# A hybrid encoder step on one core: the first query block's low products, the engines of the low parts, and the last norm

## The chip, the core and the metric

The kernel runs on one core of a Trainium2 chip. Its engines are TensorE (PE in the rows; PEld is its weight load), VectorE (DVE), ScalarE (ACT), GpSimd (POOL) and SyncE (SP), which here only issues transfers. The metric is the time of one execution on the device in microseconds; less is better.

## What is computed

One layer of a streaming encoder: 1024 prompt tokens and 128 sample tokens go through one projection to the queries, keys and values of three kinds of attention and to a gate; M is attention into 256 memory tokens, A is banded, B differential. The mixed result is gated, projected by `w_out`, added to the input and normalised.

```python
a_q, a_k, a_v, b_q, b_k, b_v, m_q, gate = split(x @ w_in)
mk, mv = split(mem_prompt @ w_mem_kv)
o_a, o_b, o_m = band(a_q, a_k, a_v), diff(b_q, b_k, b_v), memory(m_q, mk, mv)
y = (concat(o_a, o_b, o_m) * silu(gate)) @ w_out
out = layer_norm(2 ** 0.25 * x + y, g, b)      # mean and variance over 1024 features
```

## The kernel before

Every large product is made of three products of rounded numbers: an operand is split into a high part, its copy rounded to the type of the matrix product, and a low part, the rest. A product is then high by high, low by high and high by low. `step` (L154 to L157) issues these three for one of the eight slices of 128 features, `k`: L155 is x's high part with the weights' high part, L156 x's **low** part with the weights' high part, L157 x's high part with the weights' low part. ScalarE makes the high parts (a cast), VectorE or GpSimd the low parts (a subtraction).

The 1152 tokens (prompt, then sample) are three chunks of 384: `xh[c]` and `xl[c]` are x's high and low parts of chunk `c` (the last two slices of chunk 0 are in tiles named `rh` and `rl`). `load_x` (L241) brings a chunk in four transfers of two slices each, into six buffers `xr`; a buffer is free for a later transfer when both the cast and the subtraction of its slices are done. In the text these low parts are xl0a to xl0d, xl1a to xl1d and xl2a to xl2d, in the order of their transfers (xl0d is `rl`). `XP` sends the second and the fourth of each chunk to GpSimd, the others to VectorE.

The program starts with the memory's keys and values: `load_mem_w` (L221) loads and splits their weights and the memory tokens (`memr`, in the `xr` buffers too), `mem_block` (L249) makes four blocks of 256 columns. `split_mem` (L192) then splits the first unit's keys (into `ka`, `kl`) and values (`va`); its three subtractions are VectorE's.

Then comes the first query block, M0's: `q_of(units[0])` gives three chunks of eight steps; after the last step of a chunk `evac` moves the result out of its PSUM buffer `pp` (two of these) into `qa`, by ScalarE (L168) and VectorE (L172) in turn, half by half. While M0's attention runs, the projection of the next block (B0's queries, by the same `step`) fills TensorE.

A scheduler sets the order of the instructions on each engine by a model of their times; inside a `manual_schedule` block the named engine keeps the order of the code, and `high_priority` moves instructions ahead by a number of places. An engine works off its order strictly, so an instruction that waits holds up all behind it on its engine.

SyncE issues x's transfers, the next weights (`wraw`), the stores of the memory's keys and values, the tables `cos` and `sin`, and `dlam` (L307), 128 KB into a tile `t` that takes the room of what was loaded early. VectorE's row L310 works on that tile and stands ahead of the maxima (L766) that M0's softmax begins with.

At the end seven output tiles of 128 tokens follow one another: eight slices of `products` per cut, then `add` (L1052) with its statistics and `norm` (L1065). For the last tile, `t == 8`, there is nothing behind the norm to hide it: VectorE works on columns 0 to 799 (L1077, L1088); columns 800 to 1023 go to ScalarE (L1084, with a `bias` that VectorE makes first at L1083) and then through two operations of GpSimd (L1085, L1086). Both parts wait for `rstd`, a power on GpSimd (L1073). Two transfers of SyncE (L1090) store them.

## Time and profile before

| | |
|---|---|
| median of 3 runs | 676.22 us (675.5 to 677.12) |
| the profiled execution, its own time | 675.73 us |
| its span, first to last instruction | 673.9 us |
| TensorE busy | 660.9 us, 98% of the span |
| VectorE, ScalarE, GpSimd busy | 70%, 53%, 35% |
| mean granted TensorE clock | 0.996 |

The profiled execution's own time is 1.8 us above its span. In the rows below a line is: start, duration, engine, line of the kernel, operation, what it writes from what it reads, shapes and count; in square brackets the idle time of the engine ahead of it and what ended that. The busy time of TensorE is that of pipelined matrix products with modelled ends, so a product of 384 columns is shown with 0.34 us though the next starts 0.17 us later; starts are the better measure.

### The profile page before, as it was taken

Reading aid. Unit: us, or ns where it says so; the run is one execution under the profiler, and the core shown is the slowest. Engines: PE = TensorE matmul, PEld = TensorE weight load, DVE = VectorE, ACT = ScalarE, POOL = GpSimd, SP = SyncE. Lnnn points to the kernel's source line nnn. Section 1 sums busy time; section 2 is a strip of 40 time slices with the busy share of each in tenths; the row PEclk is TensorE's granted clock in tenths of the full one; section 3 lists DMA queues with packets and bytes.
Section 4 is the critical chain, followed back from the end, with each engine's and each line's share of the span. In section 5 each row is a group of like instructions: output and inputs, shape, how many; then the busy total and the mean of one; then the engine's idle time right before and its main releaser. Section 6 shows DMA issues by size and latency. Waiting matters only on the chain.

```text
span 673.9 us, 12216 instructions
## 1 busy us (share of the span) xinstructions
PE 660.9 (98%) x4306; PEld 614.8 (91%) x4306; DVE 473.7 (70%) x1169; ACT 356.3 (53%) x922; POOL 235.1 (35%) x282
## 2 busy tenths in 40 slices
PE   9899999999999999999999999999999999999995
PEld 8899999999999999999999999999999998887884
DVE  4869966796569856898466516675376689897854
ACT  6748855566455655566465635666466577211000
POOL 8654212541344333541234234313324124153101
PEclk9999999999999999999999999999999999999998
DMA  8771442022312222023322122031322657974411
GB/s 279 236 226 52 143 140 72 33 80 75 96 58 83 75 100 75 25 97 127 94 68 71 52 95 75 25 118 62 127 87 95 211 173 243 318 268 148 157 62 63
DMA packets 55693, 78.91 MB, mean 117 GB/s; under 512 B 9368, under 2 KB 33232, under 8 KB 55632
## 3 DMA queue, kind: packets, MB, share of 16 engines
q1 hardware_dynamic: 55632, 78.13, 35.4%
q8 instruction: 34, 0.56, 0.3%
q14 instruction: 27, 0.22, 0.1%
HBM read 57.69 MB, written 20.42 MB: 116 GB/s over the span
## 4 chain that ended last, share of the span: by engine, by line
PE 85%; DVE 7%; DMA 4%; issue 1%; ACT 1%; SPq 1%; POOL 0%; POOLq 0%; DVEq 0%; ACTq 0%
PE pp L155 16%; PE pp L156 16%; PE pp L157 16%; PE pp L1049 8%; PE ps L1049 6%; PE pt L476 4%; PE po L639 4%; PE ps L463 4%; PE ps L464 4%; PE po L678 3%; PE pt L891 1%; PE ps L806 1%; DVE xl L219 1%; DVE p L545 1%; PE pt L427 1%
## 5 line engine op out<-in xcount | busy, mean ns | idle before, releaser
L155 PE MATMUL pp<-xh,whi 128*128 128x384 f32 x616 | 211.5, 343 | 0.2 <-DVE qa L172 0.2
L156 PE MATMUL pp<-xl,whi 128*128 128x384 f32 x616 | 209.8, 341 | 1.8 <-DVE xl L219 1.8
L157 PE MATMUL pp<-xh,wlo 128*128 128x384 f32 x616 | 209.8, 341 | 0.0
L156 PEld LDWEIGHTS pp<-xl,whi 128*128 128x128 f32 x616 | 115.9, 188 | 4.6 <-DVE xl L219 2.4
L155 PEld LDWEIGHTS pp<-xh,whi 128*128 128x128 f32 x616 | 115.9, 188 | 3.2 <-issue 0.7
L157 PEld LDWEIGHTS pp<-xh,wlo 128*128 128x128 f32 x616 | 115.9, 188 | 1.6 <-issue 0.2
L140 POOL TENSOR_TENSOR wlo<-wraw,whi 128x512 fp32r<-128x512 f32 x54 | 72.4, 1362 | 65.6 <-ACT whi L139 50.4
L605 ACT ACTIVATE p<-ps,nm 128x512 f32<-128x512 f32 (+3 forms) x96 | 55.2, 580 | 47.8 <-DVE nm L602 36.2
L463 PE MATMUL ps<-ka,qa 128*128 128x512 f32 (+4 forms) x176 | 58.7, 339 | 0.5 <-DVE nm L712 0.5
L464 PE MATMUL ps<-kl,qa 128*128 128x512 f32 (+4 forms) x176 | 57.5, 328 | 0.0
L476 PE MATMUL pt<-ident,p 128*128 128x128 f32 x332 | 54.9, 274 | 0.6 <-DVE p L545 0.5
L600 DVE TENSOR_REDUCE nm<-ps 128x1 f32<-128x512 f32 (+3 forms) x96 | 51.0, 549 | 1.6
L480 DVE TENSOR_TENSOR ptl<-pt,pth 128x512 fp32r<-128x512 f32 x56 | 38.3, 684 | 10.3 <-ACT pth L479 9.7
L479 ACT CAST pth<-pt 128x512 fp32r<-128x512 f32 x56 | 32.6, 587 | 23.1 <-PE pt L476 19.9
L720 POOL TENSOR_SCALAR p<-p,rs 128x640 f32<-128x640 f32 (+4 forms) x32 | 21.5, 676 | 64.3 <-DVE rs L719 58.7
L476 PEld LDWEIGHTS pt<-ident,p 128*128 128x128 f32 x332 | 39.7, 141 | 3.9 <-DVE p L545 0.8
L1049 PE MATMUL pp<-xh,whi 128*128 128x512 f32 (+1 forms) x96 | 36.5, 381 | 0.0
L1049 PE MATMUL pp<-xl,whi 128*128 128x512 f32 (+1 forms) x96 | 36.2, 377 | 0.0
L1049 PE MATMUL pp<-xh,wlo 128*128 128x512 f32 (+1 forms) x96 | 35.9, 378 | 0.0
L639 PE MATMUL po<-pth,va 128*128 128x256 f32 (+1 forms) x160 | 35.4, 285 | 0.0
L463 PEld LDWEIGHTS ps<-ka,qa 128*128 128x128 f32 x176 | 33.2, 189 | 2.0 <-DVE nm L712 0.7
L484 DVE TENSOR_TENSOR ptl<-pt,pth 128x256 fp32r<-128x256 f32 (+1 forms) x72 | 25.1, 352 | 13.6 <-ACT pth L483 13.0
(240 smaller groups left out, 1425.0 us busy)
## 6 DMA issues: line engine op xcount, KB each, us to landing
wraw<-in_win SPq DMA_DIRECT2D x54, 256.0 KB, 3.2
xr<-in_xT SPq DMA_DIRECT2D x12, 384.0 KB, 4.6
gates<-t SPq DMA_DIRECT2D x24, 192.0 KB, 2.1
qa<-in_xn SPq DMA_DIRECT2D x9, 512.0 KB
out_y<-qa SPq DMA_DIRECT2D x16, 256.0 KB, 2.3
mixed<-od SPq DMA_DIRECT2D x28, 128.0 KB, 1.8
p<-gates SPq DMA_DIRECT2D x7, 512.0 KB
p<-mixed SPq DMA_DIRECT2D x7, 448.0 KB
```

The lines of the kernel that those rows point to most:

```text
L140: eng.tensor_tensor(out=lo[:, h], in0=raw, in1=f(hi[:, h]), op=ALU.subtract)
L155: nc.tensor.matmul(ps, lhsT=w[0][:, k], rhs=xh_[:, k], start=(k == 0), stop=False)
L156: nc.tensor.matmul(ps, lhsT=w[0][:, k], rhs=xl_[:, k], start=False, stop=False)
L157: nc.tensor.matmul(ps, lhsT=w[1][:, k], rhs=xh_[:, k], start=False, stop=(k == KT - 1))
L463: nc.tensor.matmul(ps, lhsT=u.qa[h][:, qs], rhs=u.ka[h][:, k0 : k0 + n], start=True, stop=False)
L464: nc.tensor.matmul(ps, lhsT=u.qa[h][:, qs], rhs=kl[h][:, k0 : k0 + n], start=False, stop=True)
L476: nc.tensor.transpose(pt[:, t, q * P : (q + 1) * P], p[q][:, cols[t][q] : cols[t][q] + P], ident)
L480: nc.vector.tensor_tensor(out=lo, in0=pt, in1=f(hi), op=ALU.subtract)
L600: nc.vector.tensor_reduce(out=nm[:, m, c : c + 1], in_=ps[c][:, : b - a], axis=AX.X, op=ALU.max, negate=True)
L605: nc.scalar.activation(e[:, a:b], ps[c][:, : b - a], AF.Exp, bias=nm[:, m, 0:1], accum_out=rs[:, m, c : c + 1])
L639: nc.tensor.matmul(out, lhsT=a, rhs=b, start=(g == 0 and x == 0), stop=(g == j and x == len(mm) - 1))
L1049: nc.tensor.matmul(y, lhsT=a[:, k], rhs=b[k][:, s], start=(k == 0 and x == 0), stop=(k == KT - 1 and x == 2))
```

## The change

There are three edits.

1. The first query block gets a function of its own, `q_first`. For each chunk it issues first the sixteen products with x's high part (`high`), and the eight with its low part (`low`) after the sixteen of the next chunk. Its third chunk has its PSUM buffer from the pool `ps_s` (three buffers, for scores), so that all three exist at once. Each of the two is a `manual_schedule` block of its own; between blocks the scheduler decides.
2. All twelve low parts of x are VectorE's, with a high priority. The three subtractions of the first memory keys and values go to GpSimd. The first transfer of the memory tokens is issued by ScalarE, not SyncE.
3. The last norm is cut into columns 0 to 383, 384 to 767 (VectorE) and 768 to 1023: there VectorE takes the mean off and multiplies by the gain, ScalarE multiplies by `rstd`, GpSimd adds; ScalarE issues the store of that part, SyncE the other two. The `bias` goes.

```diff
-XP = [2, 6]
-LS = 800
+XPR = 200
+LS = [(0, 384), (384, 768)]
...
-    def split_mem(u, kv, v):
+    def split_mem(u, kv, v, eng=nc.vector):
...
-        split_k(kv, 256, u.ka, kl, 0)
+        split_k(kv, 256, u.ka, kl, 0, eng)
...
-        nc.vector.tensor_tensor(out=u.va[:, :, :, 64:128], in0=v, in1=f(u.va[:, :, :, 0:64]), op=ALU.subtract)
+        eng.tensor_tensor(out=u.va[:, :, :, 64:128], in0=v, in1=f(u.va[:, :, :, 0:64]), op=ALU.subtract)
...
-                    nc.sync.dma_start(memr, d["memT"][:, 256 * a : 256 * b].rearrange("p (k c) -> p k c", c=256))
+                    (nc.sync if i else nc.scalar).dma_start(memr, d["memT"][:, 256 * a : 256 * b].rearrange("p (k c) -> p k c", c=256))
...
-                split_part(xh[c], xl[c], xr, a, a + 2, nc.gpsimd if a in XP else nc.vector)
+                with tc.high_priority(offset=XPR):
+                    split_part(xh[c], xl[c], xr, a, a + 2, nc.vector)
...
+    def q_first(u):
...
+        ps = [ps_p.tile([P, CH], F32, tag="pp") for _ in range(2)] + [ps_s.tile([P, 512], F32, tag="ps")[:, 0:CH]]
+        def high(c):
+            with tc.manual_schedule(engines={PE}):
+                for k in range(KT):
+                    for i in range(2):
+                        nc.tensor.matmul(ps[c], lhsT=w[i][:, k], rhs=xh[c][:, k], start=(k == i == 0), stop=False)
+        def low(c):
+            with tc.manual_schedule(engines={PE}):
+                for k in range(KT):
+                    nc.tensor.matmul(ps[c], lhsT=w[0][:, k], rhs=xl[c][:, k], start=False, stop=(k == KT - 1))
+            with tc.high_priority(offset=HP):
+                evac(c, ps[c])
+        high(0)
+        for c in range(1, 3):
+            high(c)
+            low(c - 1)
+        low(2)
...
-            bias = small.tile([P, 1], F32, tag="ri")
-            nc.vector.scalar_tensor_tensor(out=bias, in0=mv[:, 0:1], scalar=-1.0, in1=rstd, op0=ALU.mult, op1=ALU.mult)
-            nc.scalar.activation(z[:, s], z[:, s], AF.Identity, bias=bias, scale=rstd)
-            nc.gpsimd.tensor_tensor(out=z[:, s], in0=z[:, s], in1=norms[0][:, s], op=ALU.mult)
-            nc.gpsimd.tensor_tensor(out=z[:, s], in0=z[:, s], in1=norms[1][:, s], op=ALU.add)
...
+            nc.scalar.activation(z[:, rest], z[:, rest], AF.Copy, scale=rstd)
+            nc.gpsimd.tensor_tensor(out=z[:, rest], in0=z[:, rest], in1=norms[1][:, rest], op=ALU.add)
...
+        if last:
+            nc.scalar.dma_start(o["y"][t, :, rest], z[:, rest])
```

TensorE, where chunk 0 of the first query block ends (`pp_453` is chunk 0's result, `pp_508` before and `pp_454` now chunk 1's; `whi` and `wlo` are the weights' parts). Before:

```order
L155 MATMUL pp_453<-rh_24_120,whi_208 128x384
L155 MATMUL pp_508<-xh_27_123,whi_208 128x384
L156 MATMUL pp_453<-rl_26_122,whi_208 128x384
L157 MATMUL pp_453<-rh_24_120,wlo_209 128x384
L155 MATMUL pp_453<-rh_24_120,whi_208 128x384
L156 MATMUL pp_453<-rl_26_122,whi_208 128x384
L157 MATMUL pp_453<-rh_24_120,wlo_209 128x384
L156 MATMUL pp_508<-xl_28_124,whi_208 128x384
L157 MATMUL pp_508<-xh_27_123,wlo_209 128x384
```

The same place now:

```order
L993 MATMUL pp_453<-rh_24_120,whi_208 128x384
L993 MATMUL pp_453<-rh_24_120,wlo_209 128x384
L998 MATMUL pp_453<-xl_25_121,whi_208 128x384 x6
L993 MATMUL pp_454<-xh_27_123,whi_208 128x384
L993 MATMUL pp_454<-xh_27_123,wlo_209 128x384
L993 MATMUL pp_454<-xh_27_123,whi_208 128x384
L993 MATMUL pp_454<-xh_27_123,wlo_209 128x384
L998 MATMUL pp_453<-rl_26_122,whi_208 128x384 x2
L993 MATMUL pp_454<-xh_27_123,whi_208 128x384
```

Six of chunk 0's low products stand right behind its high ones and two behind four products of chunk 1; chunk 1's first low product, second in its chunk before, now stands behind all sixteen high ones, and chunk 2's eight behind its sixteen, with the first two products of the next block between the sixth and the seventh.

VectorE over the same stretch (`xl_25`/`rl_26`, `xl_28` and `xl_30` are the low parts of chunks 0, 1 and 2; `qa<-pp` is the evacuation). Before:

```order
L219 TENSOR_TENSOR xl_25_121<-xr_218,xh_23_119 128x768
L182 TENSOR_TENSOR kl_21_112<-memkv_66_259,ka_89_403 64x256
L182 TENSOR_TENSOR kl_22_113<-memkv_66_259,ka_90_404 64x256
L255 COPY memkv_74_345<-pp_320 128x256
L219 TENSOR_TENSOR xl_25_121<-xr_226,xh_23_119 128x768
L197 TENSOR_TENSOR va_411<-memv_72_318,va_411 128x4x64
L219 TENSOR_TENSOR xl_28_124<-xr_352,xh_27_123 128x768
L219 TENSOR_TENSOR xl_28_124<-xr_360,xh_27_123 128x768
L172 SCALAR_TENSOR_TENSOR qa_99_502<-pp_453,qa_99_502 64x384
```

Now:

```order
L219 TENSOR_TENSOR xl_25_121<-xr_218,xh_23_119 128x768
L219 TENSOR_TENSOR xl_25_121<-xr_222,xh_23_119 128x768
L256 COPY memkv_74_345<-pp_320 128x256
L219 TENSOR_TENSOR xl_25_121<-xr_226,xh_23_119 128x768
L219 TENSOR_TENSOR rl_26_122<-xr_230,rh_24_120 128x768
L219 TENSOR_TENSOR xl_28_124<-xr_352,xh_27_123 128x768
L219 TENSOR_TENSOR xl_28_124<-xr_356,xh_27_123 128x768
L219 TENSOR_TENSOR xl_28_124<-xr_360,xh_27_123 128x768
L219 TENSOR_TENSOR xl_28_124<-xr_364,xh_27_123 128x768
L172 SCALAR_TENSOR_TENSOR qa_101_505<-pp_453,qa_101_505 64x384
```

Chunk 0 and chunk 1 now take eight low parts of VectorE in a row, with one copy between them, where four stood with three subtractions of the memory's keys and values.

SyncE behind the last transfer of x (`t<-in_dlam` is the tile that VectorE's L310 waits for). Before:

```order
L294 DMA tab_31_127<-in_cos 128x1152
L295 DMA tab_32_128<-in_sin 128x1152
L307 DMA t_92_430<-in_dlam 128x256
L824 DMA kc_1132<-in_cmk 128x1024
L151 DMA wraw_445<-in_win 128x512
L151 DMA wraw_449<-in_win 128x512
```

Now:

```order
L295 DMA tab_31_127<-in_cos 128x1152
L296 DMA tab_32_128<-in_sin 128x1152
L151 DMA wraw_445<-in_win 128x512
L308 DMA t_92_430<-in_dlam 128x256
L151 DMA wraw_449<-in_win 128x512
L828 DMA kc_1078<-in_cmk 128x1024
```

The `dlam` transfer has moved behind the first of the next weights' transfers, which waits until GpSimd has made the low part of the first half of B0's query weights out of the buffer that it takes.

## Rows read from the trace of the kernel before

**Rows 1.** Stretch, length; busy PE, PEld, DVE, ACT, POOL; clock, DMA share, GB/s

```profile
60.00:666.00 606.00, 604.79 (x3981) 562.12 (x3979) 428.98 (x1083) 317.77 (x842) 192.42 (x235) 1.00 0.33 108
```

**Rows 2.** Timeline of TensorE, first query block: start, us, engine, line, operation

```profile
21.08 0.42 PE L155 MATMUL pp<-xh,whi 128*128 128x384 f32 x1
...
28.04 0.45 PE L156 MATMUL pp<-xl,whi 128*128 128x384 f32 x1 [1.63 <-DVE xl L219]
...
38.52 0.34 PE L155 MATMUL pp<-xh,whi 128*128 128x384 f32 x1
...
41.17 0.34 PE L155 MATMUL pp<-rh,whi 128*128 128x384 f32 x1
```

**Rows 3.** Timeline of VectorE over the first query block

```profile
18.61 0.95 DVE L219 TENSOR_TENSOR xl<-xr,xh 128x768 fp32r<-128x768 f32 x1
...
25.40 5.09 DVE L219 TENSOR_TENSOR xl<-xr,xh 128x768 fp32r<-128x768 f32 x2
30.52 0.55 DVE L172 SCALAR_TENSOR_TENSOR qa<-pp,qa 64x384 fp32r<-64x384 f32 x1
31.11 0.96 DVE L219 TENSOR_TENSOR xl<-xr,xh 128x768 fp32r<-128x768 f32 x1
...
33.22 1.97 DVE L219 TENSOR_TENSOR xl<-xr,xh 128x768 fp32r<-128x768 f32 x1 [0.57 <-ACT xh L218]
```

**Rows 4.** GpSimd: its low parts of x (min/median/max ns), two timeline rows

```profile
L219 POOL TENSOR_TENSOR xl<-xr,xh x5: 1847/2004/2199, 20.8 to 34.7; 128x768 fp32r<-128x768 f32 x5
...
36.85 2.54 POOL L140 TENSOR_TENSOR wlo<-wraw,whi 128x512 fp32r<-128x512 f32 x2
...
60.01 1.54 POOL L170 TENSOR_TENSOR qa<-t,qa 64x256 fp32r<-64x256 f32 x2 [1.00 <-ACT qa L168]
```

**Rows 5.** SyncE's issues of x's eighth and twelfth transfer, and of dlam

```profile
23.52 0.33 SPq L244 DMA_DIRECT2D xr<-in_xT  x1
...
30.52 0.33 SPq L244 DMA_DIRECT2D xr<-in_xT  x1
...
37.53 0.33 SPq L307 DMA_DIRECT2D t<-in_dlam  x1
```

**Rows 6.** ScalarE: the casts of chunk 0's second and third transfer, and the eighth

```profile
19.91 1.57 ACT L218 CAST xh<-xr 128x768 fp32r<-128x768 f32 x2
...
26.76 0.83 ACT L218 CAST xh<-xr 128x768 fp32r<-128x768 f32 x1 [1.49 <-DMA xr<-in_xT]
```

**Rows 7.** VectorE at the first row behind dlam; TensorE's wait in M0's attention

```profile
43.48 0.36 DVE L310 TENSOR_TENSOR t<-t 128x64 f32<-128x64 f32 x2 [3.24 <-DMA wraw<-in_win]
...
50.03 0.55 PE L476 MATMUL pt<-ident,p 128*128 128x128 f32 x3 [0.53 <-DVE p L545]
```

**Rows 8.** The end: timeline of all engines behind the last product

```profile
668.82 0.16 DVE L1083 SCALAR_TENSOR_TENSOR ri<-nm,rs 128x1 f32<-128x1 f32 x1 [0.44 <-POOL rs L1073]
...
669.01 0.57 ACT L1084 ACTIVATE qa<-qa,ri,rs 128x224 f32<-128x224 f32 x1 [24.51 <-DVE ri L1083]
669.66 0.79 POOL L1085 TENSOR_TENSOR qa<-qa,tab 128x224 f32<-128x224 f32 x1 [0.88 <-ACT qa L1084]
670.53 0.65 POOL L1086 TENSOR_TENSOR qa<-qa,ka 128x224 f32<-128x224 f32 x1
...
671.21 0.33 SPq L1090 DMA_DIRECT2D out_y<-qa  x1
```

**Rows 9.** The start: ScalarE's first cast of the memory, and TensorE near 13 us

```profile
4.24 0.62 ACT L218 CAST memh<-xr 128x512 fp32r<-128x512 f32 x1 [0.72 <-DMA xr<-in_memT]
...
12.62 0.41 PE L156 MATMUL pp<-meml,qa 128*128 128x256 f32 x1
12.83 0.37 PE L157 MATMUL pp<-memh,qa 128*128 128x256 f32 x1
13.04 0.28 PE L155 MATMUL pp<-memh,qa 128*128 128x256 f32 x1
13.16 0.28 PE L156 MATMUL pp<-meml,qa 128*128 128x256 f32 x1
```

More of the change, by code (lines that the diff above doesn't have):

```diff
@@ L173, in split_q, with split_k @@
                     out=qa[h][x, c0 : c0 + n], in0=src[r, 0:n], scalar=scale, in1=f(hi), op0=ALU.mult, op1=ALU.subtract)
-    def split_k(src, n, ka, kl, c0):
+    def split_k(src, n, ka, kl, c0, eng=nc.vector):
         for h in range(2):
@@ L181, in split_k @@
             nc.scalar.copy(ka[h][x, c0 : c0 + n], src[r, 0:n])
-            nc.vector.tensor_tensor(
+            eng.tensor_tensor(
                 out=kl[h][r, c0 : c0 + n], in0=src[r, 0:n], in1=f(ka[h][r, c0 : c0 + n]), op=ALU.subtract)
@@ L296, in hybrid_step @@
         units = [setup(*n) for n in names]
-        split_mem(units[0], kvs[0], mem0[0].rearrange("p t (h e) -> p t h e", h=2))
+        split_mem(units[0], kvs[0], mem0[0].rearrange("p t (h e) -> p t h e", h=2), nc.gpsimd)
     tmp = pool("tmp", 2)
@@ L369, in rope, with q_evac @@
         return t1
-    def q_block(u, blk, scale):
+    def q_evac(u, scale):
         def evac(c, ps):
@@ L384, in evac, with q_block @@
                     nc.scalar.activation(u.sqz[m][r], src[r, n:CH], AF.Copy, scale=sc)
-        return project(blk, evac)
+        return evac
+    def q_block(u, blk, scale):
+        return project(blk, q_evac(u, scale))
     def k_block(u, blk, out, skip):
@@ L976, in q_of @@
         return q_block(u, base[u.kind][0] + u.idx, -0.125 if u.kind == "A" else 0.125)
+    def q_first(u):
+        evac = q_evac(u, 0.125)
+        load_next()
+        w = loaded[base[u.kind][0] + u.idx]
+        ps = [ps_p.tile([P, CH], F32, tag="pp") for _ in range(2)] + [ps_s.tile([P, 512], F32, tag="ps")[:, 0:CH]]
[15 more added lines that the diff above has]
+        low(2)
     def k_of(u):
@@ L1073, in norm @@
         nc.gpsimd.tensor_tensor(out=rstd, in0=rstd, in1=mhalf[:, 0:1], op=ALU.pow)
-        cuts = [slice(0, LS), slice(LS, 1024)] if last else [slice(*c) for c in CUTS]
-        on_dve = cuts[:1] if last else cuts
-        for s in on_dve:
+        cuts = [slice(*c) for c in (LS if last else CUTS)]
+        rest = slice(LS[-1][1], 1024)
+        for s in [rest, slice(0, rest.start)] if last else cuts:
             nc.vector.scalar_tensor_tensor(
@@ L1079, in norm @@
         if last:
-            s = cuts[1]
-            bias = small.tile([P, 1], F32, tag="ri")
-            nc.vector.scalar_tensor_tensor(out=bias, in0=mv[:, 0:1], scalar=-1.0, in1=rstd, op0=ALU.mult, op1=ALU.mult)
-            nc.scalar.activation(z[:, s], z[:, s], AF.Identity, bias=bias, scale=rstd)
-            nc.gpsimd.tensor_tensor(out=z[:, s], in0=z[:, s], in1=norms[0][:, s], op=ALU.mult)
-            nc.gpsimd.tensor_tensor(out=z[:, s], in0=z[:, s], in1=norms[1][:, s], op=ALU.add)
-        for s in on_dve:
+            nc.scalar.activation(z[:, rest], z[:, rest], AF.Copy, scale=rstd)
+            nc.gpsimd.tensor_tensor(out=z[:, rest], in0=z[:, rest], in1=norms[1][:, rest], op=ALU.add)
+        for s in cuts:
             nc.vector.scalar_tensor_tensor(out=z[:, s], in0=z[:, s], scalar=rstd, in1=norms[1][:, s], op0=ALU.mult, op1=ALU.add)
@@ L1155, in hybrid_step @@
     late = []
-    first = [q_of(units[0])] + [gate_block(next(gates)) for _ in range(NG[0])]
-    for row in zip(*first):
-        for part in row:
-            emit(part)
+    q_first(units[0])
     for i, u in enumerate(units):
```

## The prediction

> **What bounds the kernel now.** Read first the busy time by stretch: from 60 to 666 us TensorE is busy 604.79 of 606.00 us [rows 1]. No edit shortens that work, so a gain can only come from the two ends, and what the start gains comes out at the end as long as the other engines keep up. The second view is TensorE's timeline over the first query block. From 38.52 us nothing holds it up for a while, and fifteen products of 384 columns take until 41.17: 0.177 each [rows 2]; I use 0.175. From the block's first product at 21.08 to 38.52 there are 75 such products (72 of the block, three of the next), six score products of 256 columns at 0.12 [the spacing in rows 9] and four small transposes, some 0.25 in all: 13.1 + 0.7 + 0.25 = 14.1 us. It takes 17.4. So 3.3 us are lost; the one large piece is the wait of 1.63 us for a low part ahead of 28.04 [rows 2], the rest are shorter waits and slow restarts behind them. The third view, VectorE and GpSimd over the same time, gives the cause: a low part of 768 columns takes VectorE 0.95 and 0.96 us where GpSimd is idle (18.61, 31.11), but 1.97 beside it and two together 5.09 [rows 3]; GpSimd needs 2.0 for one [rows 4]. The fourth view is the end: behind the last product a chain over VectorE, GpSimd, ScalarE, GpSimd twice and a transfer issued at 671.21 [rows 8].
>
> **The first query block.** Laid out without waits from 21.08, the new order puts TensorE at these points: chunk 0's high products to 23.2, transposes to 23.4, four more to 24.1; its fifth low product (which needs xl0c) at 24.8, xl0d at 25.9; chunk 1's sixteen high products end at 28.3, where xl1a is first wanted, and xl1d is wanted at 29.4; chunk 2's sixteen (and four score products) run from 29.7 to 33.0; xl2d is wanted at 34.4, and the third product of the next block, the equal of the point before 38.52, ends at 34.9.
>
> Now VectorE's side, at 0.95 a piece. xl0a starts at 18.61 as before; now GpSimd's two key pieces lie beside it. Such a piece (64 rows by 256) is not in the trace on GpSimd; the nearest row is 0.77 each [60.01 in rows 4], so xl0a ends between 19.6 (no contention) and 20.5. xl0b cannot begin before its cast, which is the first of two from 19.91 and ends near 20.7 [rows 6]: 21.65. The copy of the last memory block, 0.4: 22.05. xl0c 23.0, xl0d with GpSimd's value piece beside it (0.7 to 1.3 by the same rows) 24.0 to 24.9, xl1a to xl1c 25.9, 26.8, 27.8, xl1d 28.7. Each is there before it is wanted, xl1d by 0.7, xl0d by 1.0.
>
> The transfers must keep pace. The eighth transfer of x was issued at 23.52 [rows 5] and its cast began at 26.76 [rows 6], 3.24 later. It now waits for xl0b's buffer, free at 21.65, so it lands near 24.9 (the seventh waits for xl0a's buffer, so it goes at most 0.9 later than before, still ahead of the eighth); the twelfth, issued at 30.52 before [rows 5], waits for xl1b's and goes at 26.8. The cast of chunk 2's last quarter then ends near 31.7; TensorE wants it at 32.3. The next weights follow by some four microseconds earlier too.
>
> xl2: an evacuation half on VectorE costs 0.55 [rows 3]. After 28.7: half, xl2a, xl2b, half, xl2c, half, so xl2d begins at 33.2. By then GpSimd makes the next weights' low parts (two of 1.27 [rows 4], from about 32.7), so xl2d costs 1.97 as at 33.22 [rows 3], not 0.95: it ends at 35.2, 0.8 after it is wanted. I take that wait. The price of the wait is bounded by 0 (0.95 a piece) and 1.6 (2.6, half of the 5.09, with the start 0.15 later).
>
> Sum: the third product of the next block ends at 34.9 + 0.8 = 35.7. Before it was 38.52, with one pair of score products more (0.24) that now comes later. Gain 38.52 - 0.24 - 35.7 = **2.6 us**, between 1.4 and 3.4.
>
> Here the Trainium skill has a stricter rule than my rows: "SBUF — State Buffer", section "Who interferes with whom", says that VectorE, with two inputs from SBUF, and GpSimd take one pair of ports by turns, and that the later one stands still for the other's whole instruction. The 1.97 beside GpSimd against 0.95 alone agrees with turns. By that rule the three pieces that go to GpSimd would hold VectorE up by their whole lengths, 0.77 + 0.77 + 0.9 = 2.4 us instead of my 1.8, and xl1d would come at 29.3, still before 29.4; the sum would be the same, with nothing to spare.
>
> **The start.** ScalarE issues the first memory transfer, so SyncE's queue of loads is 0.4 us shorter. But the first cast in ScalarE's order is now the memory's, which began at 4.24 on arrival [rows 9], and the weights' stands behind it; it stood ahead. If the arrival is as late as before, the first product comes 0.4 later; if it gains the 0.4 of SyncE, nothing changes there and the later loads come 0.4 sooner. I take 0, between +0.4 and -0.4.
>
> **Up to 60 us.** M0's softmax hangs on VectorE's row behind the `dlam` transfer: issued 37.53 [rows 5], used at 43.48 [rows 7]. It now stands behind a weights' transfer which waits for GpSimd's first low part of B0's weights, by my times done near 34; the stores ahead of it go out four microseconds sooner. So `dlam` is issued near 34 and lands, after the same six microseconds, near 40: 3.5 sooner, when TensorE is 2.6 sooner. The wait of 0.53 at 50.03 [rows 7] then stays or goes; I take 0, between -0.5 and 0.
>
> **The end.** `rstd` is there at 668.8 (VectorE's bias begins at 668.82). The bias of 0.16 goes, so ScalarE starts at 668.85 instead of 669.01. Its 256 columns for 224 cost 0.57 x 256/224, at most 0.65: 669.5. One GpSimd operation goes, 0.87 from start to start (669.66 to 670.53); the other, 0.65 alone and 0.79 beside VectorE [all rows 8], costs 0.75 to 0.9 for 256 columns: 670.4 with the hand-over. So the last store is issued near 670.4 instead of 671.21, 0.8 sooner; VectorE's two parts are stored before it and the store itself is of about the same size (128 against 112 KB). What an issue costs on ScalarE is in no row; SyncE's is 0.33 [rows 8], and I take the same. Gain **0.8 us**, between 0.3 and 1.2.
>
> **Sum.** -2.6 + 0 + 0 - 0.8 = -3.4. Against the profiled execution's own 675.73 that is 672.3; that execution is 0.5 below the median of the runs, 676.22, so against the median **672.8 us**.
>
> **The rivals.**
>
> *Given back in M0's attention.* TensorE arrives 2.6 sooner, but its third chunk of B0's queries needs the buffer of the first, which VectorE frees only behind `dlam`. If that transfer still lands near 43.3 (it is now chained to GpSimd and to the weights' buffer), VectorE's rows do not move, and the wait at 50.03 grows by up to 2.6. Left is the end, 0.8, and up to half of the start: 674.1 to 675.4. For it speaks the new place on SyncE; against it that all that is ahead of it comes sooner.
>
> *VectorE is too slow: slower than before.* Of the twelve low parts on one engine all must be there by 38.5 less two products for no loss: from 18.61, 12 d + 3 x 0.55 + 0.4 = 38.2 - 18.6, so d = 1.46 us decides. Were each to cost 1.97, the last would come near 44.3, six microseconds late against before; less the end, 676.2 + 6 - 0.8 = 681.4. Half of the rows of before show such prices, but all beside GpSimd, which now has three small pieces and the weights there. A mean of 1.6 would give 677.1.
>
> *A new order later.* The scheduler sets the middle of the program anew. Before, all waits from 60 to 666 us are 1.2 us [rows 1]; one or two new ones of a microsecond give 674 to 675.
>
> *More than forecast.* No wait for xl2d, the wait at 50.03 gone, the start 0.4 sooner, the end 1.2: 670.5. In the same direction: products of 256 columns stood 0.21 us apart up to 12.83 and 0.12 from 13.04 on [rows 9], the lower and the higher of TensorE's two clock levels, 1.2 and 2.4 GHz, after warming products and the first memory block with gaps. If the memory arrives in fewer pieces and the clock rises sooner, each microsecond gains 0.4. The Trainium skill, "TensorE: Matmul & The Clock Gate", section "What's actually happening", has the moment of the rise vary from run to run; no row here shows a second moment.
>
> *The cover is not there.* The change removes the wait and nothing moves, because the 1.63 us only hid a later wait: within 0.2%. I see no such wait in the rows.
>
> **Chances.** Forecast (671.7 to 673.8) 0.55; more (670.5 to 671.7) 0.13; given back 0.15; a new order 0.08; VectorE too slow 0.06; nothing 0.03. A measurement of this kernel can tell about 0.2%, 1.35 us, from no change. Faster by more than that, under 674.87, are the first two, two thirds of the third and half of the fourth: 0.82; within it 0.11; slower 0.07. Leaving out what lies above 675.2 and below 670.7 leaves out less than 2 in 10: the range is 670.7 to 675.2.
>
> **What would show it.** Right: no idle of TensorE ahead of chunk 1's first low product, low parts of 0.95 each where GpSimd is idle, a short wait for xl2d, the third product of B0's queries ending near 35.7, the row that waits for `dlam` near 40, and at the end ScalarE's scaling 0.16 sooner behind `rstd`, one GpSimd operation behind it and the last store issued some 0.8 sooner behind the last product than before. Wrong: low parts of 1.5 us and more with GpSimd idle; B0's queries begun sooner but the transposes of M0's probabilities still near 50; new waits of a microsecond behind 60 us; or an end in which a store of VectorE's columns comes last.

## The result and the profile after

The changed kernel takes 670.73 us (median of 6 runs, 669.8 to 674.07), the kernel before 676.89 beside it (6 runs): a ratio of 0.9921, 95% interval 0.9897 to 0.9945. The forecast was 672.8, between 670.7 and 675.2. The time lies 0.03 us inside the lower end of that range. The gain is 6 us where 3.4 were forecast, so terms of the sum were wrong. The profiled execution took 670.51 with a span of 668.7 (before: 673.9).

TensorE's timeline over the first query block, as in [rows 2]:

```profile
19.78 0.43 PE L993 MATMUL pp<-xh,whi 128*128 128x384 f32 x1
...
20.91 0.44 PE L993 MATMUL pp<-xh,whi 128*128 128x384 f32 x1 [0.18 <-ACT xh L218]
...
30.96 0.44 PE L993 MATMUL ps<-xh,whi 128*128 128x384 f32 x1 [0.18 <-ACT xh L218]
...
32.53 0.44 PE L993 MATMUL ps<-xh,whi 128*128 128x384 f32 x1 [0.37 <-ACT xh L218]
...
35.24 0.34 PE L155 MATMUL pp<-xh,whi 128*128 128x384 f32 x1
```

The row at 35.24 is the equal of 38.52 in [rows 2], apart from one pair of score products (0.24). TensorE waits for no low part any more; what it waits for are casts of x's high parts (L218). Behind them stand VectorE, GpSimd, SyncE and ScalarE, as in [rows 3 to 7]:

```profile
18.44 0.96 DVE L219 TENSOR_TENSOR xl<-xr,xh 128x768 fp32r<-128x768 f32 x1 [1.06 <-ACT xh L218]
...
23.84 4.10 DVE L219 TENSOR_TENSOR xl<-xr,xh 128x768 fp32r<-128x768 f32 x4
...
32.57 0.96 DVE L219 TENSOR_TENSOR xl<-xr,xh 128x768 fp32r<-128x768 f32 x1
...
40.22 1.10 DVE L311 TENSOR_TENSOR t<-t 128x64 f32<-128x64 f32 x2 [3.25 <-DMA wraw<-in_win]
```

```profile
18.80 2.01 POOL L182 TENSOR_TENSOR kl<-memkv,ka 64x256 fp32r<-64x256 f32 x2 [0.57 <-ACT ka L180]
...
33.08 2.85 POOL L140 TENSOR_TENSOR wlo<-wraw,whi 128x512 fp32r<-128x512 f32 x2 [8.56 <-ACT whi L139]
```

```profile
11.43 15.13 SPq L244 DMA_DIRECT2D xr<-in_xT  x12
...
35.29 0.33 SPq L308 DMA_DIRECT2D t<-in_dlam  x1
```

```profile
31.65 0.83 ACT L218 CAST xh<-xr 128x768 fp32r<-128x768 f32 x1 [0.23 <-DMA xr<-in_xT]
```

Eleven of the twelve low parts take 0.94 to 0.96 us. Of the four in a row (4.10) the first, from 23.84, takes 1.50: GpSimd's value piece (L197, 23.04 to 24.52) lies beside it. Before, those beside GpSimd took up to 1.97, and 5.09 for two. `dlam` is used at 40.22, 3.26 sooner than in [rows 7], and the wait at 50.03 is gone.

The end, as in [rows 8]; the last matrix product started at 660.67 (before 665.76), so from there to the end of the span (668.72 and 673.92 in the traces) it is 8.05 us against 8.16:

```profile
662.17 0.15 DVE L1102 TENSOR_SCALAR rs<-nm 128x1 f32<-128x1 f32 x1
662.24 1.40 DVE L1107 SCALAR_TENSOR_TENSOR qa<-qa,nm,tab 128x256 f32<-128x256 f32 x2
662.76 1.29 POOL L1103 TENSOR_TENSOR rs<-rs,mhalf 128x1 f32<-128x1 f32 x1 [10.11 <-DVE qa L1107]
664.09 0.51 ACT L1111 ACTIVATE qa<-qa,rs 128x256 f32<-128x256 f32 x1 [24.66 <-POOL rs L1103]
...
664.67 1.14 POOL L1112 TENSOR_TENSOR qa<-qa,ka 128x256 f32<-128x256 f32 x1 [0.62 <-ACT qa L1111]
...
665.84 0.35 ACTq L1118 DMA_DIRECT2D out_y<-qa  x1
```

Where the time went over the program, by progress: the time at which TensorE had started a given share of its columns, counted from the traces (4306 matrix products in each). The products stand in another order in each kernel, so an entry can be compared to some 0.3 us. At 4.3% (57,856 columns) the kernel before is at its row of 38.52, just behind the first query block; the last column is the start of the last product.

```
                                 4.3%     12%     80%    100%
before                          38.52   90.58  539.36  665.76
changed                         35.59   84.90  533.15  660.67
changed, second execution       37.14   86.61  534.85  661.82
e1 products alone               38.45   90.73  539.57  666.42
e2 engines alone                35.54   85.50  535.49  662.41
e3 norm alone                   39.16   91.95  540.53  668.19
e4 first load alone             38.45   90.81  539.34  666.29
e8 changed, wide rest           35.02   84.60  532.86  659.84
e10 e8 with 7 buffers           34.77   84.09  532.32  659.42
e11 e8, old product order       35.40   85.23  533.61  662.37
e12 before, dlam early          40.29   90.26  541.97  668.59
e13 e10 with dlam early         35.67   84.94  535.13  661.85
```

Of the 5.1 us up to the last product 2.9 are there just behind the first block; 2.8 more come between there and 12%, 0.5 between 12 and 80%; 1.1 are given back between 80 and 100%; the end gives 0.1. The part given back is no larger than the difference between executions: `e3` has the same matrix products in the same order as the kernel before and takes 127.66 us from 80 to 100%, the kernel before 126.40, the changed one 127.52.

### The profile page after: what moved, and what is told of

Same layout as the page of the kernel before. It is cut to its first block, busy times and chain, and to the rows that moved or that the text cites. A ratio compares the mean times of both kernels' runs of the same rounds, so it can differ in the third digit from the quotient of the medians.

```text
span 668.7 us, 12238 instructions
## 1 busy us (share of the span) xinstructions
PE 655.7 (98%) x4306; PEld 611.3 (91%) x4306; DVE 464.4 (69%) x1173; ACT 355.4 (53%) x922; POOL 224.1 (34%) x278
## 4 chain that ended last, share of the span: by engine, by line
PE 87%; DMA 4%; DVE 4%; ACT 2%; issue 2%; SPq 1%; POOLq 0%; POOL 0%; DVEq 0%; ACTq 0%
PE pp L155 16%; PE pp L156 16%; PE pp L157 16%; PE pp L1079 8%; PE ps L1079 6%; PE pt L480 5%; PE po L643 4%; PE ps L467 4%; PE ps L468 4%; PE po L682 3%; DMA xr<-in_xT 2%; PE pt L895 1%; PE ps L810 1%; PE pt L431 1%; DMA xr<-in_memT 1%
## 5 line engine op out<-in xcount | busy, mean ns | idle before, releaser
L155 PE MATMUL pp<-xh,whi 128*128 128x384 f32 x594 | 204.3, 344 | 0.0
L156 PE MATMUL pp<-xl,whi 128*128 128x384 f32 x594 | 202.4, 341 | 0.0
L157 PE MATMUL pp<-xh,wlo 128*128 128x384 f32 x594 | 202.3, 341 | 0.0
L155 PEld LDWEIGHTS pp<-xh,whi 128*128 128x128 f32 x594 | 111.8, 188 | 2.3 <-DVE t L454 0.4
L156 PEld LDWEIGHTS pp<-xl,whi 128*128 128x128 f32 x594 | 111.8, 188 | 1.9 <-issue 0.2
L157 PEld LDWEIGHTS pp<-xh,wlo 128*128 128x128 f32 x594 | 111.7, 188 | 1.7 <-issue 0.2
L139 ACT CAST whi<-wraw 128x512 fp32r<-128x512 f32 x54 | 30.9, 618 | 7.4 <-PE pp L156 3.8
```

What stands on the lines that cost most here:

```text
L155: nc.tensor.matmul(ps, lhsT=w[0][:, k], rhs=xh_[:, k], start=(k == 0), stop=False)
L156: nc.tensor.matmul(ps, lhsT=w[0][:, k], rhs=xl_[:, k], start=False, stop=False)
L157: nc.tensor.matmul(ps, lhsT=w[1][:, k], rhs=xh_[:, k], start=False, stop=(k == KT - 1))
```

## The experiments

**Four parts of the change, each alone on the kernel before.** The first: the products in the new order, all else as before.

```
-    first = [q_of(units[0])] + [gate_block(next(gates)) ...]
+    q_first(units[0])
```

> The kernel before with one part of the change alone: the first query block's low products a chunk later; x's low parts stay where they were (some on GpSimd), and so do the start and the end. Theory 1 (the gain needs both the later products and the low parts on VectorE): a later low product can only use a low part that is there; GpSimd's pieces beside VectorE cost 1.97 to 2.5 each, so the last low part of chunk 2 is hardly earlier than before. Waits move rather than go: the product behind the third of the next block ends 0.5 to 1.2 us sooner than the 38.52 us of before, and the time falls by 0.5 to 1.2 us (ratio .9982 to .9993). Rival (the order of the products is all that matters): it ends 1.7 us sooner in relation to the first x product, and the time falls by about 2 us (.997). Rival clock (the rise of TensorE's clock is a matter of the execution, not of the change): the spacing of the 256-column products goes from 0.21 to 0.12 us at moments that differ between the executions, between about 5 and 13 us, whatever part of the change a kernel has.

677.35 us against 676.81: ratio 1.001 (0.9996 to 1.0024). TensorE's timeline:

```profile
30.51 0.62 PE L997 MATMUL pp<-xl,whi 128*128 128x384 f32 x2 [1.34 <-DVE xl L219]
...
37.56 0.34 PE L156 MATMUL pp<-xl,whi 128*128 128x384 f32 x1
38.17 0.44 PE L157 MATMUL pp<-xh,wlo 128*128 128x384 f32 x1 [0.27 <-POOL wlo L140]
...
47.14 0.33 PE L479 MATMUL pt<-ident,p 128*128 128x128 f32 x1
48.13 0.39 PE L466 MATMUL ps<-ka,qa 128*128 128x256 f32 x1 [0.66 <-ACT p L771]
```

TensorE now waits for chunk 1's third low part (xl1c) instead of its first; VectorE ends it where it did before (30.5, [rows 3]). The product behind the third of the next block starts at 37.56 instead of 38.52 (with one pair of score products, 0.24, fewer ahead of it), so theory 1 is right there; but at once TensorE waits for GpSimd's low part of the next weights (38.17), at 4.3% 0.1 us is left, at 12% nothing, and the 0.5 to 1.2 us that theory 1 gave for the whole time do not come.

The second: the engines alone.

```
-    split_part(xh[c], xl[c], xr, a, a + 2, nc.gpsimd if a in XP else nc.vector)
+    with tc.high_priority(offset=XPR):
+        split_part(xh[c], xl[c], xr, a, a + 2, nc.vector)
...
-    split_mem(units[0], kvs[0], mem0[0]...)
+    split_mem(units[0], kvs[0], mem0[0]..., nc.gpsimd)
```

> The kernel before with the other part of the first block's change alone: x's low parts all on VectorE with their priority, the first memory keys' and values' low parts on GpSimd; the products stay in the old order. Theory 1: TensorE still wants each low part right behind the chunk's own high products, xl0d at about 23.2 us where VectorE has it at 24 to 25, so a wait of 1 to 1.5 us stays in chunk 0; chunk 1 and 2 follow without. The product behind the third of the next block ends 1 to 1.5 us sooner than before, time 1 to 1.5 us less (.998). Rival (order of the products is all): no change, within 0.3 us. Rival clock: as for the other runs, the moment of the rise differs by the execution and with it up to 1.3 us.

672.9 us: ratio 0.9946 (0.9927 to 0.9965). The waits of the block:

```profile
21.94 0.44 PE L156 MATMUL pp<-xl,whi 128*128 128x384 f32 x1 [0.46 <-DVE xl L219]
...
30.29 0.42 PE L155 MATMUL pp<-xh,whi 128*128 128x384 f32 x1 [0.36 <-DVE qa L172]
```

So 3.65 us come from the engines alone, more than twice what theory 1 gave, and the rival (only the order counts) falls.

The third: the last norm alone.

```
-LS = 800
+LS = [(0, 384), (384, 768)]
...
-    nc.scalar.activation(z[:, s], z[:, s], AF.Identity, bias=bias, scale=rstd)
+    nc.scalar.activation(z[:, rest], z[:, rest], AF.Copy, scale=rstd)
```

> The kernel before with the new last norm alone (ScalarE takes 256 columns without a bias, one GpSimd operation less, its part stored by ScalarE). By the prediction's own step: 0.8 us sooner (.9988). By what the changed kernel's trace shows (GpSimd's power on rstd ends 0.41 us behind VectorE's last subtraction, as it did before, and rstd comes 0.36 later for it): the time from the last product to the end of the span is 7.75 against 7.85 us, so 0.1 us sooner, not to be told from no change.

676.86 us: ratio 1.0002 (0.9988 to 1.0015). Yet here the end is 7.57 us long, 0.6 less than before:

```profile
669.69 0.15 DVE L1072 TENSOR_SCALAR rs<-nm 128x1 f32<-128x1 f32 x1
669.76 1.40 DVE L1077 SCALAR_TENSOR_TENSOR qa<-qa,nm,tab 128x256 f32<-128x256 f32 x2
669.99 0.66 POOL L1073 TENSOR_TENSOR rs<-rs,mhalf 128x1 f32<-128x1 f32 x1 [9.82 <-DVE rs L1072]
670.68 0.51 ACT L1081 ACTIVATE qa<-qa,rs 128x256 f32<-128x256 f32 x1 [23.73 <-POOL rs L1073]
```

The same power takes 0.66 where the changed kernel shows 1.29: here it starts 0.23 us behind VectorE's first subtraction (669.76) and ends between the two; there it starts 0.52 behind it and ends behind the second. 0.6 us lies inside the interval of the times, so the times can't confirm it.

The fourth: the first memory transfer issued by ScalarE.

```
-    nc.sync.dma_start(memr, d["memT"]...)
+    (nc.sync if i else nc.scalar).dma_start(memr, d["memT"]...)
```

> The kernel before with one line changed: the first transfer of the memory's columns is issued by ScalarE instead of SyncE. If this is what makes TensorE's clock rise sooner (the memory arrives sooner, the warming products and the memory's products follow more closely), the 256-column products stand 0.12 us apart from 5 to 7 us on instead of from 13 us, the first x product comes 1.3 us sooner and the time falls by about 1.3 us (.998). If the moment of the rise is the execution's own, or the rest of the change's, the products stand 0.21 apart until 13 us as before, and the time is that of before, or up to 0.5 us more since the weights' cast then stands behind the memory's (first product 5.4 us instead of 4.9).

676.34 us: ratio 1.0002 (0.9989 to 1.0016), with the same order of matrix products as before:

```profile
19.57 0.42 PE L155 MATMUL pp<-xh,whi 128*128 128x384 f32 x1
...
22.66 0.45 PE L156 MATMUL pp<-xl,whi 128*128 128x384 f32 x1 [1.23 <-POOL xl L219]
...
27.97 0.45 PE L156 MATMUL pp<-xl,whi 128*128 128x384 f32 x1 [1.65 <-DVE xl L219]
```

The first x product comes 1.5 us sooner than in [rows 2], and a new wait of 1.23 for GpSimd's low part takes it back: the product behind the long wait starts at 27.97, before at 28.04. The old block's end stands with the low parts, whatever TensorE does ahead of them.

The four alone add up to 0.40% less (-0.54 + 0.10 + 0.02 + 0.02), together they make 0.79 to 0.89%.

**The moment of the clock.** The changed kernel again, unchanged; then with more warming products; and the kernel before with more.

```
-WU = 8
+WU = 12
```

> The changed kernel once more, for a second profiled execution and more times. If the rise of TensorE's clock near 5 to 6.7 us belongs to the change, its first x product starts near 19.8 us again and the ratio is .992. If it is the execution's own, this execution may show a rise at another moment, up to 13 us, with the first x product up to 1.3 us later, and the times spread over some 1.3 us or more (the six of before: 2.1 us, the six of the change: 4.3 us).

> The changed kernel with 12 warming products ahead of the first memory block instead of 8. They end at about 6.8 us instead of 4.9, so the first product of the memory block starts up to 1.4 us later than its 5.44. If the changed kernel's early rise of the clock is certain without them: slower by 0 to 1 us than the changed kernel, or the same, since the memory block waits for its transfers anyway. If the early rise is by chance and more warming makes it certain: the same median or up to 0.6 us less than the changed kernel, and a smaller spread of the times.

> The kernel before with 12 warming products instead of 8. If the late rise of the clock (13 us) costs the kernel before 1.3 us and more warming brings it forward, the 256-column products stand 0.12 us apart from 7 us on, the first x product starts near 19.8 us instead of 21.08, and the time falls by 0.8 to 1.3 us (.998 to .9988). If the moment of the rise is not moved by them, or if the x product waits for its cast anyway, no change.

671.12 us (0.9911, 0.9893 to 0.9929), 671.42 (0.9916, 0.9901 to 0.993) and 676.71 (0.9997, 0.9987 to 1.0008): more warming changes nothing that can be measured. For each profiled execution, the number of memory products that stand 0.21 us apart (the lower clock level) instead of 0.12, where there are more than four the start of the last of them, and the start of the first x product. A count of four is that of single products right behind a wait.

```
first load by SyncE    before 23, 12.83, 21.08   e3 26, 13.94, 21.71   e7 19, 14.21, 21.88   e12 24, 13.96, 21.82
                       e1 12, 11.71, 20.76   e2 12, 10.67, 20.02
first load by ScalarE  changed 4, 19.78   again 14, 9.72, 19.54   e4 4, 19.57   e6 4, 19.96
                       e8 11, 10.87, 20.21   e10 4, 19.43   e11 11, 9.91, 19.86   e13 4, 20.47
```

The moment differs between executions of one program (4 and 14 slow products), so rival "clock" is right in that. What counts is when the last slow product comes, not how many there are: the 14 of the second execution end at 9.72 and do not make it late; in the kernel before twelve stand behind 10.3 and cost 0.09 each, 1.1 us. (Where the profile shows the granted clock of such a stretch it is 0.50, as in `e8` from 8 to 11 us; in the kernel before it shows 1.00 there, so the level is read from the spacing.) With SyncE's first load the last slow product comes between 10.67 and 14.21 and the mean start is 21.2; with ScalarE's it comes by 10.87 or there is none, and the mean start is 19.9. So the sooner start goes with the change, though `e2` overlaps; why the first load moves the clock was not shown.

The second execution also shows what now ends the block, a wait of 1.76 for the cast of x's last quarter:

```profile
32.65 0.44 PE L993 MATMUL ps<-xh,whi 128*128 128x384 f32 x1 [1.76 <-ACT xh L218]
...
34.90 0.52 PE L155 MATMUL pp<-xh,whi 128*128 128x384 f32 x1
35.22 0.52 PE L156 MATMUL pp<-xl,whi 128*128 128x384 f32 x1
```

**The end, cut anew**, in the changed kernel: ScalarE and GpSimd take 384 columns, so VectorE's first subtraction is longer.

```
-LS = [(0, 384), (384, 768)]
+LS = [(0, 320), (320, 640)]
```

> The changed kernel with the last norm cut anew once more: ScalarE and GpSimd take 384 columns (640 to 1023) instead of 256, VectorE two parts of 320. VectorE's first subtraction is then 384 wide instead of 256 and lasts until about 0.5 us behind its start. Theory (GpSimd's power waits until VectorE's running two-input operation ends, and gets in between two of them only if it is issued by then): the power, issued 0.5 us behind the start, gets in behind the first subtraction, rstd comes 0.3 to 0.5 us sooner, but ScalarE's and GpSimd's 384 columns cost 0.25 and 0.4 us more: the same within 0.3 us; what tells is where the power ends, 0.4 us behind VectorE's first subtraction or again behind its second. Rival (the power is long by itself, 1.29 us): it ends 1.3 us behind its issue wherever VectorE's operations lie.

669.56 us (668.98 to 670.5): ratio 0.9892 (0.9877 to 0.9907), beside 0.9911 for the changed kernel on the same chip; the intervals overlap.

```profile
661.41 1.40 DVE L1107 SCALAR_TENSOR_TENSOR qa<-qa,nm,tab 128x384 f32<-128x384 f32 x2
661.93 0.55 POOL L1103 TENSOR_TENSOR rs<-rs,mhalf 128x1 f32<-128x1 f32 x1 [10.11 <-DVE rs L1102]
662.51 0.61 ACT L1111 ACTIVATE qa<-qa,rs 128x384 f32<-128x384 f32 x1 [23.92 <-POOL rs L1103]
```

The power starts 0.52 behind the first subtraction, as in the changed kernel, and now ends in 0.55: the rival (it is long by itself) falls. From the last product to the end of the span it is 7.76 us, in the three runs built on this one 7.76 to 7.78, against 8.04 to 8.05 in three executions with the change's own cut: 0.3 us, shown by the traces. The rest of the 1.56 us between the two medians has no row.

**What binds the block now.** The kernel of the last run with seven raw buffers, the order of instructions unchanged:

```
-XB = 6
+XB = 7
```

> The changed kernel with the last norm's wide rest (640 to 1023, as in the run before it) and seven instead of six buffers for the raw blocks of the first loads, so that each transfer of x may be issued one low part sooner; the order of the instructions on all engines is the same. In four executions of the changed kernel's start TensorE waited 0.37, 1.76, 0.79 and 0.24 us for the cast of x's last quarter (near 32 us), whose transfer comes last. Theory (that transfer now binds the first query block, and is late because it waited for a buffer): the wait is under 0.2 us, the other waits for casts of chunk 2 go too, and the time is 0.4 to 0.9 us below the same kernel with six buffers (669.56): 668.7 to 669.2. Rival (the transfer engines are full from 26 to 32 us anyway, their busy share is 0.94 to 1.03 there): the same waits, the same time within 0.3 us.

669.38 us: ratio 0.9917 (0.99 to 0.9933), on a chip on which the kernel before took 675.79.

```profile
33.80 0.61 PE L998 MATMUL ps<-xl,whi 128*128 128x384 f32 x2 [0.36 <-DVE xl L219]
```

```profile
32.03 1.71 DVE L219 TENSOR_TENSOR xl<-xr,xh 128x768 fp32r<-128x768 f32 x1
```

```profile
31.63 3.25 POOL L140 TENSOR_TENSOR wlo<-wraw,whi 128x512 fp32r<-128x512 f32 x2 [7.65 <-ACT whi L139]
```

TensorE waits for no cast any more; the last one starts at 30.20 instead of 31.08 to 32.31 in the four executions with six buffers. So that transfer did bind the block, and it was late for want of a buffer. Behind it stands the wait that the prediction gave to the change itself: the next weights come sooner too, GpSimd starts on them 0.4 us ahead of xl2d, and xl2d takes 1.71 and is waited for. At 4.3% TensorE is 0.25 us further than with six buffers, at 12% 0.5, at the last product 0.4; in the time it shows as nothing: 0.2 us by the medians, and the ratio is rather worse.

The same kernel with six buffers and the products in the old order:

```
-    q_first(units[0])
+    first = [q_of(units[0])] + [gate_block(next(gates)) ...]
```

> The changed kernel with the wide rest, but with the first query block's products in the old order: all else (engines of the low parts, first transfer, last norm) as in the change. Theory (the engines give nearly all; the order of the products saves two waits of 0.46 and 0.36 us in the block): 0.3 to 0.8 us above the new order's 669.56, so 669.9 to 670.4. Rival (the order is worth the 2.0 us by which the change beat the kernel with the new engines alone, 672.9 against 670.9): 671.3 to 671.8.

670.95 us: ratio 0.9933 (0.9919 to 0.9948) against 0.9892 (0.9877 to 0.9907) for the new order on another chip; on this chip the new order, with seven buffers, has 0.9917 (0.99 to 0.9933), and the intervals overlap. By progress the old order costs 0.4 to 0.6 us up to 12%, as the theory has it; another 1.8 are lost between 80 and 100%:

```profile
535.33 0.39 PE L467 MATMUL ps<-ka,qa 128*128 128x256 f32 x1 [0.61 <-ACT p L772]
...
567.15 0.36 PE L682 MATMUL po<-pth,va 128*128 128x256 f32 x1 [1.36 <-DVE tab L667]
```

The engines alone (e2) are level with the change at 4.3% and lose 1.7 against it elsewhere, between 12 and 80%, 0.8 of it in two waits near 176 us. The theory fits the progress, and neither fits the time: the direct worth of the order is small, and the rest lies in waits far from the block, at a different place in each order, which argues for the scheduler's later choices rather than for the edit; that was not tested apart.

**`dlam` early**, in the kernel before, and in the one with seven buffers: its transfer and the arithmetic behind it stand in the scope of the first loads.

```
-    dl = tmp.tile([P, 256], F32, tag="t2")       (behind the stores)
+        dl = ep.tile([P, 256], F32, tag="dl")    (ahead of setup)
```

> The kernel before with one thing moved: the transfer of dlam and the arithmetic behind it stand in the first loads (near 9 us) instead of behind the memory's stores, so VectorE's row of M0's softmax is not held for 3.24 us until 43.48. Between 38 and 90 us the kernel before lost about 2 us more than the changed one, in waits of 0.3 to 0.8 us for M0's and B0's probabilities. Theory (those are the price of VectorE's row standing behind dlam): they go, and the time falls by 1.5 to 2.3 us, to 674.4 to 675.2, though the 1.63 us for the low part stay. Rival (they come from VectorE's later work as a whole, which the low parts put off; dlam hides beside TensorE's products): no change within 0.6 us.

> The changed kernel with wide rest and seven buffers, and dlam early as in the kernel before it. VectorE stood still for 3.25 us ahead of dlam in the changed kernel as well (until 40.22), but TensorE had no wait over 0.15 us behind it. Theory (in the changed kernel dlam costs nothing any more): the same as with seven buffers and dlam late, within 0.5 us. Rival (it still sets when M0's probabilities come): 0.5 to 1.5 us less.

678.91 us, slower: ratio 1.0045 (1.0032 to 1.0058); and 671.67, ratio 0.9943 (0.9929 to 0.9958), 2.3 us above the same kernel with `dlam` late. Both miss. In the first, M0's transposes need no wait, and from 4.3% to 12% it takes 49.97 us where the kernel before takes 52.06, so the theory's 2 us are there. But at 4.3% it is 1.8 us later: its first x product starts 0.74 later, and a new wait for a low part stands ahead of the old one:

```profile
24.24 0.44 PE L156 MATMUL pp<-xl,whi 128*128 128x384 f32 x1 [0.74 <-POOL xl L219]
...
29.55 0.44 PE L156 MATMUL pp<-xl,whi 128*128 128x384 f32 x1 [1.64 <-DVE xl L219]
```

and 3 us are lost between 12 and 80%, against 0.5 won there by the change; `e13`, too, loses 2.0 there against the same kernel with `dlam` late, and 0.9 at 4.3%. What loses it was not tested apart: the transfer and six rows of VectorE stand ahead of x's low parts, and the order of the whole program is another. As built, moving `dlam` costs more than it gives.

## Why the prediction held, just, and which of its terms were wrong

The time lies in the range by 0.03 us, and that is luck: the sum left out 2.7 us that came up to 12%, and the time stayed in the range only because the end fell 0.7 short and 1.1 were lost late in the program. It is the case "more than forecast" (0.13) that came, with three of its four signs.

*The first block, forecast 2.6.* From the first x product to the row that answers 38.52 it is 15.46 us against 17.44; less the score pair that is 1.74. The wait of 1.63 is gone, and the low parts came nearly as laid out: 0.95 each, and of the two places where GpSimd was to hold VectorE up only the second did (1.50 beside the value piece, 0.55 more, on xl1a instead of xl0d). Nor did VectorE's first piece reach to 20.5: it started first (18.44) and took 0.96, while the key piece beside it (18.80) took 1.20 and the next, alone, 0.74. What failed is the step on xl2d: it starts at 32.57, ahead of GpSimd's weights (33.08), keeps its 0.96, and was not waited for; GpSimd's first half took 1.61 instead of 1.29. The wait is a true mechanism where GpSimd starts first, as `e10` shows (1.71 for the 1.97 of the prediction, a wait of 0.36). The step on the transfers, by which chunk 2's last cast would end at 31.7, ahead of TensorE's need, failed the other way: it ends at 32.48. It was waited for in all four executions with the new engines, the new order and six buffers, by 0.37, 1.76, 0.79 and 0.24 us.

*The start, forecast 0.* The first x product came 1.30 sooner. The bound of 0.4 looked at the issue alone; the price of the lower clock level, which stood among the rivals ("each microsecond gains 0.4"), was left out of it. It is not a gain to be added, though: e4 has it and gains nothing, since the low parts were late; and with the new engines the end of the block goes with x's last transfer (first x products at 19.54, 19.78 and 20.21 gave 37.14, 35.59 and 35.02 at 4.3%).

*Up to 60 us, forecast 0 to 0.5.* The largest error: 2.7 us between 4.3% and 12%. `dlam` moved as forecast (40.22 for "near 40") and the wait at 50.03 went. But the kernel before loses time behind it too, which I overlooked: starts that come late among M0's and B0's transposes of probabilities. The prediction took the stretch from 60 us on as full because TensorE is busy in 604.79 of its 606.00 us; the late start at 62.00 lies in it, and busy time with modelled ends hides it. TensorE's timeline, first before, then changed:

```profile
61.19 0.90 PE L476 MATMUL pt<-ident,p 128*128 128x128 f32 x4
62.00 0.39 PE L463 MATMUL ps<-ka,qa 128*128 128x256 f32 x1
```

```profile
59.21 0.60 PE L480 MATMUL pt<-ident,p 128*128 128x128 f32 x4
59.56 0.42 PE L155 MATMUL pp<-xh,whi 128*128 128x384 f32 x1
```

From the transposes to the next product it is 0.81 before and 0.35 now, the figure of every undisturbed group of four. So 0.46 is lost there and 0.77 at 50.03 (set against products that follow closely; the idle time in [rows 7] is 0.53 of it), 1.2 us together; the changed kernel has no start there over 0.2 us late. The rest of the 2.7 is in small pieces, part of them the order's own: in the kernel before transposes stand right ahead of products of L806 three times (69.20, 76.32, 77.14), which costs some 0.2 us each time in every run that has it, with `dlam` early too, and the changed kernel has no such place up to 12%.

Two things changed together. VectorE's row was 3.26 sooner, as TensorE was; and TensorE has more to do before it needs M0's probabilities: from the first x product to the first transpose of `p` the kernel before starts 52,096 columns (e1 48,896), the changed one 55,168. That is eight products of 384, 1.4 us of cover. It comes with the new engines, not with the order of the first block: `e2` and `e11`, in the old order, have 55,168 too. Every kernel run with 55,168 has no start over 0.3 us late there but one (0.42 in e2), each with 52,096 and fewer has two or more of 0.3 to 0.9, apart from those with `dlam` early (35,840 and 40,704), which have none but ahead of L806. So the cover agrees with all where `dlam` comes late; a kernel in which it alone was changed was not run. The rival "given back in M0's attention" did not come, and e1 does not show it either: most of its gain was lost at 38.17, ahead of that attention, to GpSimd's low part of the next weights.

*The end, forecast 0.8, got 0.1.* The step "`rstd` is there at 668.8" failed: it took the power's place as fixed. VectorE's subtraction in two pieces and a start 0.52 behind it made ScalarE's scaling start 1.92 us behind the row that adds epsilon (662.17), where 668.85 would have been 1.59 behind it (before 667.26), and the addition on GpSimd took 1.14 beside VectorE's scaling, not 0.75 to 0.9. So the last store is issued 0.28 sooner behind the last product (5.17 against 5.45), and from its issue to the end of the span it is 2.88 instead of 2.71, so that 0.1 is left. In e3 the power gets in between and the end is 0.6 shorter.

*A new order later* is not shown: the 1.1 us given back behind 80% are within what executions of one order differ by, though there is a wait of 0.60 near 543 us that the profile of the kernel before does not have (`e3`, in the old order, has one of 0.62 near 551).

So the misses went both ways: 0.4 more than forecast at the start and the block together, 2.7 between 4.3% and 12%, 0.5 between 12 and 80%, 0.7 less at the end, 1.1 less behind 80%. Between the two profiled executions they leave 5.2 us where 3.4 were forecast; the medians differ by 6.2, since the profiled execution of before is 1.2 under the median of its six runs and the changed one 0.2.

## What to carry to other kernels

A wait removed ahead of a row that another engine serves at a fixed time only moves: here the new order and the sooner start were each worth nothing alone (677.35 and 676.34 us beside 676.81), while freeing the engine that serves the low parts was worth 3.65 us alone. Look first for the engine or transfer whose rows keep their absolute times when TensorE's move; change that one. Behind it, ask how much work TensorE has in hand before each row it will wait for, since a scheduler that orders the program anew changes this cover too, here by 3,072 columns. And compare starts, not busy time: a busy share of 99.8% hid late starts.

## What the runs showed of the hardware

The power of one column on GpSimd takes 0.55, 0.66, 0.79, 1.22 or 1.29 us (e8, e3, e11, before, changed), by whether one of VectorE's operations with two inputs from SBUF ends soon behind its start; before and after it ends 0.41 us behind the end of VectorE's subtraction (668.78 against 668.37, 664.05 against 663.64), in e3 and e11 0.41 behind the first of two. The Trainium skill, "SBUF — State Buffer", section "Who interferes with whom", has the two take one pair of ports by turns; these ends agree. So do the low parts, where the piece that starts second is the longer one: VectorE's 1.50 (23.84) behind GpSimd's value piece and 1.71 in e10 behind the weights, GpSimd's 1.20 (18.80) and 1.61 (33.08) behind VectorE's, which kept 0.96. Why the power starts 0.23 us behind the subtraction in some programs and 0.52 in others (0.52 in both executions of the changed kernel) stays open.

A wait of 1.76 us was followed by products at half the clock: in the second execution's stretches (columns as in [rows 1]) the clock is 0.50 and 0.65, and products stand 0.32 apart until 37 us. The seven from 34.90 to 37.14 alone take 1.0 us more than at 0.174.

```profile
34.00:36.00 2.00, 2.00 (x8) 2.00 (x7) 0.56 (x1) 0.20 (x1) 1.97 (x2) 0.50 0.91 344
36.00:38.00 2.00, 2.00 (x10) 2.00 (x9) 0.73 (x2) 0.76 (x2) 0.00 (x0) 0.65 1.06 372
```

In the kernel before, a wait of 1.63 was not followed by that; its products behind 28.32 stand 0.17 apart. What makes the difference is not shown.
